# Experts of a mixture layer taken two at a time, each in one column half of the PE array

## The chip, the cores and the metric

The kernel runs on one core of one Trainium2 chip. The metric is the device time of one execution in microseconds; the median of three runs counts. All weights are read from HBM once, in fp32, 363.5 MB on the queue that carries them.

## What is computed

One layer: a token mixer (Fourier branch and a recurrent branch) and then an expert-choice feed-forward part, on 512 tokens of 1024 features. The change lies in the second part alone. Cut to that:

```python
def expert_choice_ffn(h, w_router, w_gate, w_up, w_down):
    cap = CAPACITY_FACTOR * T // N_EXPERTS                 # 2 * 512 / 16 = 64 tokens
    scores = softmax(einsum('btd,de->bte', h, w_router))
    g, idx = lax.top_k(swapaxes(scores, 1, 2), cap)        # each expert picks 64 tokens
    xg = h[idx]
    hid = silu(einsum('becd,edf->becf', xg, w_gate)) * einsum('becd,edf->becf', xg, w_up)
    out = einsum('becf,efd->becd', hid, w_down) * g[..., None]
    return zeros.at[idx].add(out)

x = x + g2 * expert_choice_ffn(modulate(rmsnorm(x, norm2_g), sh2, sc2), ...)
return rmsnorm(x, final_g)
```

There are 16 experts (NE). Each has w_gate and w_up of 1024 x 1536 and w_down of 1536 x 1024.

## The kernel before

The mixer and the router take the time up to some 468 us; the change leaves the order of their instructions as it is, but for one small copy on VectorE (csv) that is there so that the tile cs can live in a pool that closes early.

**Loads.** Each of the three matrices of an expert comes in eight units of 768 KB, 128 partitions x 1536 fp32 (6 KB a row). The list `units` (L827) gives their order: expert by expert, gate, up, down. `eload()` (L835) issues the next one on SP's queue; it goes into a ring of 22 buffers, 20 of three pools (NR = 14, 5, 1) and two lent from staging tiles (wd and we; `held`). A buffer is free when the matmuls that read its old contents are done, so each `eload()` stands right behind the products of a unit. SP's transfers take eight completion lanes in turn: a load is issued only when the one eight before it has landed, and copies that ACT issues take lanes of the same set. Expert 15's down matrix comes in nine smaller pieces (`LAST`, L829; L856): 512 columns in four pieces of three k blocks, then twice 256 columns in larger and smaller ones, which makes 2 KB and 1 KB a row.

**One expert** (loop at L1160). `up_gate` (L1108, products at L1116) multiplies the gathered tokens (xg, 64 columns as the stationary operand) by a unit, the two halves f of the 1536 columns in the two column halves of the PE array (tile_position (0, 64f)), each 384 columns at a time, into a two-bank PSUM tile, G or U. After each k a list of hooks runs other work: the scatter of the expert before (L1122, 1132), and the ranking of the expert after next (rank_a L1042, rank_d on VectorE, rank_p L1059 to 1069, rank_c L1071 to 1080). Silu (L1172, ScalarE) and the product with U (L1185, VectorE) follow; six transposes T (L1198), two copies to hT (L1199), and the down products Y (L1210), 512 columns in either half. After an odd expert the gather of the next two (`gather`, L1088, 64 matmuls of 128 columns) stands ahead of the transposes. For expert 0 the gather is spread: two pieces (`one_k`) ahead of the loop, the others and those of expert 1 in hooks. The gate row g2 is brought to the partitions it is needed on by two copies at expert 2 (L1190) and one at expert 14 (L1215), both on ACT's queue.

**PSUM.** G and U have two banks each, and four one-bank buffers ("a") serve everything else.

Of the kernel before, what the change touches and what calls it, by code (L numbers as in the profile page):

```python
# [76 lines left out]
def layer(ctx: ExitStack, tc: tile.TileContext, I, out):  # L77
# [54 lines left out]
    cs = keep.tile([P, KD, 32], F32, name="cs")  # L132
# [131 lines left out]
    def ada_acc(i):  # L264
        for j in ada_at.get(i, ()):
            raw = take("a", j)
            r = [stage.tile([P, 256], F32, tag="acc", bufs=2, name=f"acc{j}_{a}") for a in range(2)]
            m = len(r)
            for k in range(KD):
                if k < m:  # L270
                    dve.tensor_scalar(r[k], raw[:, k, :], cs[:, k, 0:1], None, op0=OP.mult)
                else:
                    dve.scalar_tensor_tensor(r[k % m], raw[:, k, :], cs[:, k, 0:1], r[k % m], op0=OP.mult, op1=OP.add)
# [36 lines left out]
    zs = st_p.tile([P, NT, 1028], F32, name="zs")  # L310
    rs, ce = zs[:, 0, 0:1024], zs[:, 1, 0:512]
# [523 lines left out]
    def eload():  # L835
# [5 lines left out]
        m, i = n % (sum(NR) + 2), 0  # L841
# [9 lines left out]
        if wn == "w_down_e":  # L851
            if e == NE - 1:
# [152 lines left out]
    for _ in range(NR[1]):  # L1005
# [8 lines left out]
    jk = wa[:, 2, P:P + 256].bitcast(BF16)  # L1014
    wb = stage.tile([P, 4, 512], F32R, tag="wH", bufs=2, name="wb")
    wc = stage.tile([P, 2048], F32, tag="wL", bufs=2, name="wc")
    wd = stage.tile([P, 2048], F32, tag="wH", bufs=2, name="wd")
    we = stage.tile([P, 2048], F32, tag="wL", bufs=2, name="we")
    held += [wd[:, 0:DE], we[:, 0:DE]]
    eload()  # L1020
    eload()
    g20 = we[:, DE:2048]
    sl = wc[:, 1280:2048]
    y = sl[:, 0:512]
    half = lambda t: t.bitcast(BF16)
    eq = lambda t: half(t).rearrange("p (n t) -> p n t", n=NT)
    RK = [(sB, [half(wc[:, 256 * c:256 * c + 256]) for c in range(NT)], eq(wc[:, 1024:1280])),
          (wa[:, 3, :], [half(sl[:, 256 * c:256 * c + 256]) for c in range(3)] + [half(wd[:, DE:DE + 256])],
           eq(wd[:, DE + 256:2048]))]
    oht = [wb[:, i, :] for i in range(3)]  # L1030
    yH = wb[:, 3, :]
    yL = [stage.tile([P, 256], F32R, tag="acc", bufs=2, name=f"yL{a}") for a in range(2)]
    hT = [t.rearrange("p (a b) -> p a b", a=3) for t in (wa[:, 3, 0:384], wd[:, DE:DE + 384])]
    xg = g1.rearrange("p (k c) -> p k c", k=KD)

    def at(name, shape=(P, 512)):
        return mps.tile(list(shape), F32, tag="a", bufs=4, name=name)

    def bcast(col4):
        a = at("bc")  # L1040
        for n in range(NT):
            pe.transpose(a[:, P * n:P * n + P], col4(n).to_broadcast([P, P]), ident)  # L1042
        return a

    def rank_a(e):
# [13 lines left out]
    def rank_p(e):  # L1059
        sB, GT, EQ = RK[e == 1]  # L1060
# [7 lines left out]
        h = CAP * (e % 2)  # L1068
        dve.tensor_tensor(oh[:, :, h:h + CAP], r.unsqueeze(2).to_broadcast([P, NT, CAP]),
                          iota0[:, None, :].to_broadcast([P, NT, CAP]), op=OP.is_equal)  # L1070

    def rank_c(e):
        sB, GT, EQ = RK[e == 1]
        a = at("rb")
        for c in range(NT - 1):
            pe.matmul(a, onesb, GT[c], start=c == 0, stop=False)
        for c in range(NT):
            pe.matmul(a[:, P * c:P * c + P], onesb, EQ[:, c, :], start=False, stop=False)
        pe.matmul(a, onesb, GT[NT - 1], start=False, stop=True)
        dve.tensor_scalar(oht[e % 3], a, pmod, None, op0=OP.is_equal)  # L1080
        dve.scalar_tensor_tensor(jk, oht[e % 3].bitcast(F32), 1.0, sB, op0=OP.mult, op1=OP.mult,
                                 accum_out=gc[:, e % 3:e % 3 + 1])

    h0, h1, hh = slice(0, CAP), slice(CAP, P), slice(0, P)

    def gather_k(a, k, q):
        for n in range(NT):
            pe.matmul(a[k // 4][:, P * (k % 4) + q.start:P * (k % 4) + q.stop], XN[n // 2][:, n % 2, P * k:P * k + P],  # L1088
                      oh[:, n, q], start=n == 0, stop=n == NT - 1)

    def gather_out_k(a, k, q):
        src = a[k // 4][:, P * (k % 4) + q.start:P * (k % 4) + q.stop]
        if k % 2 or k < 3 and q == h0:
            act.activation(xg[:, k, q], src, AF.Identity, bias=modc[:, 24 + k, 0:1], scale=s2[:, k:k + 1])
        else:
            dve.tensor_scalar(xg[:, k, q], src, s2[:, k:k + 1], modc[:, 24 + k, 0:1], op0=OP.mult, op1=OP.add)

    def gather():
        a = [at("xg0"), at("xg1")]
        for k in range(KD):  # L1100
            gather_k(a, k, slice(0, P))
        return a

    def gather_out(a, q):
        for k in range(KD):
            gather_out_k(a, k, q)

    def up_gate(e, wn, name, hooks):  # L1108
# [230 lines left out]
```

## Time and profile before

| | |
|---|---|
| runs | 1208.59, 1205.56, 1209.94 us, median 1208.59 |
| profiled execution | 1205.73 us, span 1203.9 us, mean granted clock 0.984 |
| busy, share of the span | PE 95%, VectorE 47%, ScalarE 24%, GpSimd 9% |
| transfers | 368 MB, mean 306 GB/s over the span |
| the experts | from the first product at 482.3 us to the last output |

In the page's forty slices (30 us each) the bandwidth is 356 GB/s in the slice from 570 us, then 418 to 422 in each up to 1140, 400 in the next and 211 in the last. TensorE is at 90% and more in nearly all slices, so the page's first line alone does not tell what the time hangs on. Rows are read as: line of the program, engine, operation, output <- inputs, shape, count, busy time. A matmul in fp32 leaves two records, so a product that the program writes once is counted twice.

### The profile page before, as it was taken

The page shows a single profiled execution, that of the slowest core. Times are in us where ns is not written, and L with a number is a line of the kernel's source. Part 1 is how long each engine was busy: PE and PEld are TensorE (multiplying, and loading weights), DVE is VectorE, ACT ScalarE, POOL GpSimd, SP SyncE. Part 2 cuts the span into 40 slices and gives each one's busy share as a digit, 9 for nine tenths or more (in the row PEclk, how much of TensorE's full clock was granted, in tenths as well). Part 3 has the DMA queues.
Part 4 walks back from the last instruction along what each step waited for, and adds up shares of the span by engine and source line. Part 5 has one row for each costly group of instructions (what it writes and reads, how often), then busy time and mean ns, then how long its engine had stood idle before and what let it go on. Part 6 is the DMA issues. An engine that isn't in the chain of part 4 may idle for free. (4 is left out here: it accounts for less than half of the span.)

```text
span 1203.9 us, 16716 instructions
## 1 busy us (share of the span) xinstructions
PE 1148.4 (95%) x6891; PEld 684.3 (57%) x6891; DVE 564.3 (47%) x1053; ACT 286.4 (24%) x448; POOL 112.9 (9%) x118
## 2 busy tenths in 40 slices
PE   8979988899999999999999999999999999999986
PEld 5768766588888897545445445445345345345333
DVE  5566899996776675233332332332232232232024
ACT  5443766644322223101001001001001001001004
POOL 5164443310000000000000000000000000000002
PEclk9989988999999999999999999999999999999998
DMA  8922011155555495899899999999999999999995
GB/s 308 300 89 88 18 53 53 35 173 177 188 180 191 149 390 206 313 379 418 356 422 419 418 420 421 418 419 421 420 417 421 421 418 418 422 421 418 419 400 211
DMA packets 115435, 368.01 MB, mean 306 GB/s; under 512 B 8912, under 2 KB 61656, under 8 KB 115232
## 3 DMA queue, kind: packets, MB, share of 16 engines
q1 hardware_dynamic: 112688, 363.52, 76.9%
q0 software_dynamic: 1088, 2.18, 0.6%
q10 hardware_dynamic: 1584, 1.25, 0.4%
q8 instruction: 54, 0.88, 0.3%
q14 instruction: 21, 0.17, 0.0%
HBM read 364.43 MB, written 2.10 MB: 304 GB/s over the span
## 5 line engine op out<-in xcount | busy, mean ns | idle before, releaser
L1116 PE MATMUL U<-ew,g 128*64 128x384 f32 x928 | 167.5, 494 | 8.7 <-DMA ew<-in_w_up_e 8.6
L1116 PE MATMUL G<-ew,g 128*64 128x384 f32 x960 | 171.7, 493 | 3.8 <-DMA ew<-in_w_gate_e 3.5
L1135 DVE TENSOR_TENSOR x<-x,sc 128x512 f32<-128x512 f32 x120 | 77.1, 684 | 104.2 <-PE sc L1132 104.2
L1116 PEld LDWEIGHTS G<-ew,g 128*64 128x64 f32 x960 | 62.8, 136 | 87.0 <-issue 62.6
L1116 PEld LDWEIGHTS U<-ew,g 128*64 128x64 f32 x928 | 60.0, 136 | 90.6 <-issue 56.9
L1247 POOL TENSOR_TENSOR o<-x,ew 128x512 f32<-128x512 f32 (+1 forms) x8 | 7.8, 1003 | 926.7 <-ACT o L1243 926.7
L1213 DVE SCALAR_TENSOR_TENSOR wc<-Y,gc,g 128x512 f32<-128x512 f32 x15 | 11.3, 751 | 148.6 <-PE Y L1210 148.6
L1210 PE MATMUL Y<-ew,wa 128*64 128x512 f32 x312 | 75.7, 598 | 2.2 <-ACT wa L1199 2.2
L1210 PE MATMUL Y<-ew,wd 128*64 128x512 f32 x324 | 77.5, 594 | 0.0
L1199 ACT COPY wa<-T 128x384 f32<-128x384 f32 x16 | 7.7, 479 | 254.2 <-PE T L1198 254.2
L230 DVE TENSOR_TENSOR wL<-raw,wH 128x1024 fp32r<-128x1024 f32 x48 | 62.9, 1341 | 2.0 <-ACT wH L229 1.6
L1172 ACT ACTIVATE wc<-G 128x768 f32<-128x768 f32 x16 | 13.0, 811 | 181.7 <-PE G L1116 181.7
L1210 PEld LDWEIGHTS Y<-ew,wd 128*64 128x64 f32 x324 | 24.2, 137 | 49.1 <-issue 41.7
L1088 PEld LDWEIGHTS xg<-wa,xn 128*128 128x128 f32 x448 | 51.1, 192 | 0.2
L1088 PE MATMUL xg<-wa,xn 128*128 128x128 f32 x448 | 51.2, 275 | 0.0
L1054 DVE TENSOR_SCALAR wc<-wa,score 128x128 bf16<-128x128 f32 (+3 forms) x63 | 24.0, 381 | 56.7 <-ACT wa L1047 56.7
L1210 PEld LDWEIGHTS Y<-ew,wa 128*64 128x64 f32 x312 | 21.8, 136 | 45.0 <-issue 34.6
L1216 ACT CAST wb<-wc 128x512 fp32r<-128x512 f32 x15 | 9.3, 619 | 156.1 <-DVE wc L1213 156.1
L674 PE MATMUL ga<-u,gw 128*128 128x512 f32 x64 | 36.0, 645 | 10.0 <-issue 9.9
L1132 PEld LDWEIGHTS sc<-wb 64*128 64x128 f32 x240 | 23.6, 184 | 35.9 <-issue 35.9
L229 ACT CAST wH<-raw 128x1024 fp32r<-128x1024 f32 x38 | 37.9, 1045 | 17.8 <-PE zO L426 9.9
L699 POOL TENSOR_TENSOR th<-tp,th 128x768 f32<-128x768 f32 x16 | 35.0, 2206 | 49.2 <-DVE tp L698 49.2
(360 smaller groups left out, 2183.9 us busy)
## 6 DMA issues: line engine op xcount, KB each, us to landing
ew<-in_w_gate_e SPq DMA_DIRECT2D x120, 768.0 KB, 14.9
ew<-in_w_up_e SPq DMA_DIRECT2D x116, 768.0 KB, 14.9
ew<-in_w_down_e SPq DMA_DIRECT2D x113, 768.0 KB, 14.9
raw<-in_w_ada SPq DMA_DIRECT2D x24, 1024.0 KB, 5.4
raw<-in_w_in SPq DMA_DIRECT2D x16, 1024.0 KB, 4.9
wd<-in_w_down_e SPq DMA_DIRECT2D x7, 768.0 KB, 12.3
we<-in_w_down_e SPq DMA_DIRECT2D x7, 768.0 KB, 12.9
wd<-in_w_up_e SPq DMA_DIRECT2D x6, 768.0 KB, 14.6
```

Of the source, the lines that this page charges most:

```text
L229: (copy or act.copy)(wH[:, a], raw[:, a])
L230: dve.tensor_sub(wL[:, a], raw[:, a], wH[:, a].bitcast(F32))
L674: pe.matmul(gf[:, 512:1024], gw[:, d, i, :], u[:, TC:TA], start=True, stop=True)
L699: pool.tensor_tensor(b, s, b, op=OP.mult)
L1054: dve.tensor_scalar(GT[c][:, 0:m], sB[:, 0:m], s, None, op0=OP.is_lt)
L1088: pe.matmul(a[k // 4][:, P * (k % 4) + q.start:P * (k % 4) + q.stop], XN[n // 2][:, n % 2, P * k:P * k + P], oh[:, n, q], start=n == 0, st ...
L1116: pe.matmul(t[64 * f:64 * f + 64, n, 0:384], xg[:, k, c:c + CAP], w[:, o:o + 384], start=k == 0, stop=k == KD - 1, tile_position=(0, 64 * f))
L1132: pe.matmul(a[dh][:, c], w, v, start=j == 0, stop=j == 1, tile_position=(64 * dh, 0))
L1135: dve.tensor_add(xs, xs, a[dh])
L1172: act.activation(v3(sl), G[:, :, 0:384], AF.Silu)
L1210: pe.matmul(yp[64 * dh:64 * dh + 64, :], hT[j // 3][:, j % 3, 64 * f:64 * f + 64], w[:, 512 * i:512 * i + 512], start=f == 0 and j == 0, s ...
L1213: dve.scalar_tensor_tensor(y, yp, gc[:, e % 3:e % 3 + 1], g2, op0=OP.mult, op1=OP.mult)
```

## The change

It takes the experts in pairs, p = 0 to 7, expert 2p in the lower and 2p + 1 in the upper column half.

- `units` alternates between the two experts of a pair, so a step of `up_gate` takes two units: three blocks of 512 columns for each expert. Each step issues two loads behind it. The ring has 21 buffers (we alone is lent).
- PSUM: six one-bank tiles (`mt`: three for G, three for U, then the two gather pieces, three for T, two for Y), two small ones (`at`).
- `rank_c` writes both experts of a pair into the two halves of one tile. The scatter sums both experts in one product over 128 partitions, 16 matmuls a pair of 512 columns.
- The gather of expert 0 stands as a whole ahead of the loop, and then rank_p(1) and two pieces for expert 1 (`gather_1`); the other six pieces are in the hooks of pair 0.
- The gate row copies: three on ACT's queue (`expand`) behind the gate products of pair 0; the late one is gone. The second column half of the gate row has a place of its own (g2b).
- `LAST` now holds for both experts of the last pair, 18 pieces instead of nine; the output part is adapted to it.

```diff
-    for e in range(NE):
-        units += [(e, wn, q) for wn in ("w_gate_e", "w_up_e", "w_down_e") for q in range(KD)]
+    for p in range(NE // 2):
+        units += [(2 * p + i, wn, q) for wn in ("w_gate_e", "w_up_e", "w_down_e") for q in range(KD) for i in range(2)]
...
-    units[-KD:] = [(NE, "final_g", 0)] + [(NE - 1, "w_down_e", (c0, cw, k0, nk)) for c0, cw, ks in LAST for k0, nk in ks]
+    units[-2 * KD:] = [(NE, "final_g", 0)] + [(NE - 2 + i, "w_down_e", (c0, cw, k0, nk))
+                                              for c0, cw, ks in LAST for k0, nk in ks for i in range(2)]
...
-        m, i = n % (sum(NR) + 2), 0
+        m, i = n % (sum(NR) + 1), 0
...
+    def mt(name):
+        return mps.tile([P, 512], F32, tag="m", bufs=6, name=name)
...
-    def up_gate(e, wn, name, hooks):
-        t = mps.tile([P, 2, 512], F32, tag=name, bufs=1, name=name)
-        c = CAP * (e % 2)
-        for k in range(KD):
-            w = EW.pop((e, wn, k))
-            for n in range(2):
-                for f in range(2):
-                    o = FH * f + 384 * n
-                    pe.matmul(t[64 * f:64 * f + 64, n, 0:384], xg[:, k, c:c + CAP], w[:, o:o + 384],
-                              start=k == 0, stop=k == KD - 1, tile_position=(0, 64 * f))
-            eload()
+    def up_gate(p, wn, name, hooks):
+        t = [mt(name) for _ in range(3)]
+        for k in range(KD):
+            w = [EW.pop((2 * p + i, wn, k)) for i in range(2)]
+            for b in range(3):
+                for i in range(2):
+                    pe.matmul(t[b][hf[i], :], xg[:, k, hf[i]], w[i][:, 512 * b:512 * b + 512],
+                              start=k == 0, stop=k == KD - 1, tile_position=(0, CAP * i))
+            eload()
+            eload()
...
+    def scatter(p, i):
+        n, dh = divmod(i, 2)
+        a = at("sc")
+        w = oht[p % 2][:, P * n:P * n + P]
+        for j, v in enumerate((yH[dh], yL[dh])):
+            pe.matmul(a, w, v, start=j == 0, stop=j == 1)
...
-    one_k(0, h0)
-    one_k(1, h0)
-    for e in range(NE):
+    g0 = mt("xg0")
+    for k in range(KD):
+        gather_k(g0[:, CAP * k:CAP * k + CAP], k, hf[0])
+    for k in range(KD):
+        xg_put(g0[:, CAP * k:CAP * k + CAP], k, hf[0], True)
+    rank_p(1)
+    gather_1(0)
+    gather_1(1)
+    for p in range(NP):
...
-            hooks[0] += [lambda: one_k(2, h0), lambda: rank_p(1)]
-            hooks[4].append(lambda: rank_c(0))
-            hooks[6].append(lambda: rank_c(1))
-            for k in range(3, KD):
-                hooks[k - 2].append(lambda k=k: one_k(k, hh))
+            for k in range(2, KD):
+                hooks[k - 2].append(lambda k=k: gather_1(k))
+            hooks[6].append(lambda: rank_c(0))
...
-        if e == 2:
-            for q in range(2):
-                nc.scalar.dma_start(g20[64 * q:64 * q + 64, :], g2[0:64, :])
+        if p == 0:
+            def expand():
+                for i in range(2):
+                    nc.scalar.dma_start(g2b[hf[i], :], g2[hf[1], :])
+                nc.scalar.dma_start(g2[hf[1], :], g2[hf[0], :])
+            hooks[0].append(expand)
+        Uu = up_gate(p, "w_up_e", "U", hooks)
...
-        if e == NE - 2:
-            nc.scalar.dma_start(g2[0:64, :], g2[64:128, :])
```

Three places in the order of instructions. The first is TensorE where the loop begins. Before (L1088 is the gather, xa a piece's PSUM tile, G the gate product of unit ew0):

```order
2014 L1141 MATMUL warm_3823<-onesb_87 128x512
2015 L1141 LDWEIGHTS onesb_87
2016 L1141 MATMUL warm_3823<-onesb_87 128x512
2017 L1088 MATMUL xa_3838<-wa_3345,xn2_0_3419 128x64 x2
2018 L1088 MATMUL xa_3838<-wa_3345,xn2_2_3596 128x64 x2
2019 L1088 MATMUL xa_3844<-wa_3345,xn2_0_3419 128x64 x2
2020 L1088 MATMUL xa_3844<-wa_3345,xn2_2_3596 128x64 x2
2021 L1116 MATMUL G_3850<-ew0_3168,g1_94 64x384 x4
```

Two pieces of the gather stand here between the warming matmuls and the first unit. Now, at the same place on TensorE, the end of what stands ahead of the first unit (L1068 is rank_p(1), L1094 the gather, and eight pieces of expert 0 stand ahead of that):

```order
2072 L1068 MATMUL rk_3884<-onesb_87,wb_3759 128x1
2073 L1094 MATMUL xa_3907<-wa_3347,xn2_0_3421 128x64 x2
2074 L1094 MATMUL xa_3907<-wa_3347,xn2_2_3598 128x64 x2
2075 L1094 MATMUL xa_3913<-wa_3347,xn2_0_3421 128x64 x2
2076 L1094 MATMUL xa_3913<-wa_3347,xn2_2_3598 128x64 x2
2077 L1113 MATMUL G_3919<-ew0_3170,g1_94 64x512
2078 L1113 MATMUL G_3919<-ew1_3172,g1_94 64x512
2079 L1113 MATMUL G_3920<-ew0_3170,g1_94 64x512
2080 L1113 MATMUL G_3920<-ew1_3172,g1_94 64x512
2081 L1113 MATMUL G_3921<-ew0_3170,g1_94 64x512
2082 L1113 MATMUL G_3921<-ew1_3172,g1_94 64x512
```

The first unit has moved from row 2021 to row 2077, and units ew0 and ew1, of the two experts, alternate in three blocks.

The second place is ACT's queue around the gate row copies, after the change (L1050 the copy of a rank's scores, L1171 Silu, g_95 the gate row g2, wc the tile that holds g2b):

```order
L1050 COPY wa<-bc 128x512
L1171 ACT_TABLE_LOAD
L1171 ACTIVATE wc<-G 128x512 x3
L1188 DMA wc<-g_95 64x512 x2
L1189 DMA g_95<-g_95 64x512
L1050 COPY wa<-bc 128x512
```

Before, two copies (L1190) stood behind the third expert's Silu and score copy, and one (L1215) behind the fifteenth's down product.

The third place is SP's queue at the end of the weights. Before:

```order
L847 DMA ew_7893<-in_final_g 128x1024
L856 DMA ew_7898<-in_w_down_e 128x3x512
L856 DMA ew_7903<-in_w_down_e 128x3x512
L856 DMA ew_7908<-in_w_down_e 128x3x512
L856 DMA ew_7913<-in_w_down_e 128x3x512
L856 DMA ew_7918<-in_w_down_e 128x6x256
L856 DMA ew_7930<-in_w_down_e 128x6x256
L856 DMA ew_7936<-in_w_down_e 128x6x256
L856 DMA ew_7954<-in_w_down_e 128x4x256
L856 DMA ew_7960<-in_w_down_e 128x2x256
```

Now the pieces of 512 columns are eight, and behind them stand these, two of each for the two experts:

```order
L859 DMA we<-in_w_down_e 128x6x256
L859 DMA ew_7242<-in_w_down_e 128x6x256
L859 DMA ew_7250<-in_w_down_e 128x6x256
L859 DMA ew_7252<-in_w_down_e 128x6x256
L859 DMA ew_7260<-in_w_down_e 128x6x256
L859 DMA ew_7262<-in_w_down_e 128x6x256
L859 DMA ew_7270<-in_w_down_e 128x4x256
L859 DMA ew_7272<-in_w_down_e 128x4x256
L859 DMA ew_7280<-in_w_down_e 128x2x256
L859 DMA ew_7282<-in_w_down_e 128x2x256
```

So the down matrix of expert 14, eight units of 1536 columns a row before, has moved into the list of small pieces.

## Rows read from the trace of the kernel before

**Rows 1.** Windows: stretch, us; busy PE, PEld, DVE, ACT, POOL; PEclk; DMA; GB/s

```profile
480.00:600.00 120.00, 119.49 (x822) 61.07 (x821) 38.37 (x95) 13.07 (x24) 0.00 (x0) 1.00 0.94 367
620.00:1140.00 520.00, 506.54 (x3262) 235.50 (x3258) 154.40 (x339) 43.33 (x82) 0.00 (x0) 1.00 1.02 420
1140.00:1160.00 20.00, 17.79 (x105) 6.67 (x106) 5.37 (x9) 1.43 (x2) 0.00 (x0) 1.00 1.01 403
1170.00:1175.00 5.00, 3.33 (x20) 1.57 (x18) 0.95 (x1) 0.81 (x2) 0.00 (x0) 1.00 1.02 383
1180.00:1185.00 5.00, 4.55 (x25) 2.26 (x25) 1.52 (x4) 0.62 (x1) 0.00 (x0) 1.00 0.96 311
```

**Rows 2.** The page's DMA issues: count, size, us from issue to landing

```profile
ew<-in_w_gate_e SPq DMA_DIRECT2D x120, 768.0 KB, 14.9
```

**Rows 3.** Timeline of PE at the loop's start: start us, us, instruction

```profile
479.38 0.24 PE L1065 MATMUL rk<-onesb,wc 128*128 128x1 bf16 x4
...
480.42 1.97 PE L1088 MATMUL xa<-wa,xn 128*128 128x64 f32 x16
482.32 1.51 PE L1116 MATMUL G<-ew,g 128*64 128x384 f32 x8
...
484.70 0.17 PE L1063 MATMUL rk<-onesb,wd 128*128 128x1 bf16 x1
...
485.28 1.51 PE L1116 MATMUL G<-ew,g 128*64 128x384 f32 x8
...
494.31 0.82 PE L1076 MATMUL rb<-wc,onesb 128*128 128x512 bf16 x3
...
495.40 1.05 PE L1088 MATMUL xa<-wa,xn 128*128 128x128 f32 x8
```

**Rows 4.** Timeline of PE, experts 2 to 4, last field in brackets: idle before

```profile
576.11 2.75 PE L1116 MATMUL G<-ew,g 128*64 128x384 f32 x16
...
649.23 2.79 PE L1210 MATMUL Y<-ew,wa 128*64 128x512 f32 x12 [0.17 <-ACT wa L1199]
...
659.59 2.75 PE L1116 MATMUL G<-ew,g 128*64 128x384 f32 x16
662.26 0.40 PE L1132 MATMUL sc<-wb 64*128 64x256 f32 x2
...
662.94 2.80 PE L1116 MATMUL G<-ew,g 128*64 128x384 f32 x16
```

**Rows 5.** Groups of PE instructions by line: busy us, mean ns | idle before

```profile
L1088 PE MATMUL xg<-wa,xn 128*128 128x128 f32 x448 | 51.2, 275 | 0.0
...
L1198 PE MATMUL T<-cst,wc 128*128 128x128 f32 x96 | 16.4, 307 | 2.3 <-DVE wc L1185 2.3
...
L1042 PE MATMUL bc<-cst,score 128*128 128x128 f32 x64 | 10.1, 284 | 0.1
```

**Rows 6.** SP's waits (us in total, times, longest), and SP's timeline from 580 us

```profile
SPq L861 <- DMA we<-g: 13.4, 1, 13.4
...
593.33 3.97 SPq L861 DMA_DIRECT2D ew<-in_w_gate_e  x8
```

**Rows 7.** Loads that SP issued from 496 to 504 us, line L861

```profile
DMA to landing us min/median/max: 4.1/4.1/4.3
```

**Rows 8.** The copies of L1190, that of L1215, and the page's Silu group

```profile
DMA to landing us min/median/max: 2.3/2.3/2.3
...
DMA to landing us min/median/max: 6.5/6.5/6.5
...
L1172 ACT ACTIVATE wc<-G 128x768 f32<-128x768 f32 x16 | 13.0, 811 | 181.7 <-PE G L1116 181.7
```

**Rows 9.** The last weight loads (L856), and DVE behind the last product

```profile
L856 SPq DMA_DIRECT2D ew<-in_w_down_e x9: 378/2518/3777, 1159.7 to 1181.4; - x9
...
DMA to landing us min/median/max: 7.8/12.5/14.7
...
1191.67 0.48 DVE L1274 SCALAR_TENSOR_TENSOR wc<-Y,gc,g 128x256 f32<-128x256 f32 x1 [1.04 <-PE Y L1267]
```

More of the change, by code (lines that the diff above doesn't have):

```diff
@@ L1030, in layer @@
[L1030 to L1033, printed above, removed]
+    RK = [(b, [half(wb[:, 1024 * i + 256 * c:1024 * i + 256 * c + 256]) for c in range(NT)], q)
+          for i, (b, q) in enumerate(((sB, eq(wa[:, 2, P:P + 256])), (wa[:, 3, :], eq(e1))))]
+    hT = wb[:, 0:DE].rearrange("p (a b) -> p a b", a=12)
@@ L1075, in rank_c @@
         for c in range(NT - 1):
-            pe.matmul(a, onesb, GT[c], start=c == 0, stop=False)
+            both(slice(0, T), lambda r: r[1][c], start=c == 0, stop=False)
         for c in range(NT):
[L1078 to L1082, printed above, removed]
@@ L1098, in gather @@
[L1098 to L1117 removed]
+            both(slice(P * c, P * c + P), lambda r: r[2][:, c, :], start=False, stop=False)
@@ new lines, in layer @@
+        if p:
+            for i in range(6):
+                hooks[2 + i].append(lambda i=i: scatter(p - 1, i))
+        else:
+            for k in range(2, KD):
+                hooks[k - 2].append(lambda k=k: gather_1(k))
+            hooks[6].append(lambda: rank_c(0))
+        nx = 2 * p + 2
+        if p + 1 < NP:
+            hooks[1 if p else 7].append(lambda: rank_a(nx))
+            for c in range(NT if p else 0):
+                hooks[2 + c].append(lambda c=c: rank_d(nx, c))
+            if p:
+                hooks[7].append(lambda: rank_p(nx))
@@ new lines, in layer @@
+        G = up_gate(p, "w_gate_e", "G", hooks)
+        for b in range(3):
+            act.activation(sl[:, 512 * b:512 * b + 512], G[b], AF.Silu)
+        hooks = {k: [] for k in range(KD)}
+        if p:
+            for i in range(2):
+                hooks[i].append(lambda i=i: scatter(p - 1, 6 + i))
+        elif p + 1 < NP:
+            for c in range(NT):
+                hooks[0].append(lambda c=c: rank_d(nx, c))
+            hooks[1].append(lambda: rank_p(nx))
+        if p + 1 < NP:
+            hooks[2].append(lambda: rank_a(nx + 1))
+            for c in range(NT):
+                hooks[3 + c].append(lambda c=c: rank_d(nx + 1, c))
+            hooks[7].append(lambda: rank_p(nx + 1))
@@ new lines, in layer @@
+        for a in range(3):
+            t = mt("T").rearrange("p (a b) -> p a b", a=4)
+            for b in range(4):
+                f, j = divmod(4 * a + b, 6)
+                pe.transpose(t[:, b, :], sl[:, FH * f + j:FH * f + FH:6], ident)
+            act.copy(hT[:, 4 * a:4 * a + 4, :], t)
+        if p == NP - 1:
+            break
+        Y = [mt("Y") for _ in range(2)]
+        for q in range(KD):
+            w = [EW.pop((2 * p + i, "w_down_e", q)) for i in range(2)]
+            f = q // 4
+            for b in range(3):
+                j, dh = divmod(3 * (q % 4) + b, 2)
+                for i in range(2):
+                    pe.matmul(Y[dh][hf[i], :], hT[:, 6 * f + j, hf[i]], w[i][:, 512 * b:512 * b + 512],
+                              start=f == 0 and j == 0, stop=f == 1 and j == 5, tile_position=(0, CAP * i))
+            eload()
+            eload()
@@ L1235, in out_a @@
         else:
-            for i in range(2):
-                c = slice(256 * i, 256 * i + 256)
-                pe.matmul(a[:, c], w, yH[:, c], start=True, stop=False)
-                pe.matmul(a[:, c], w, yL[i], start=False, stop=True)
+            pe.matmul(a, w, yH[0], start=True, stop=False)
+            pe.matmul(a, w, yL[0], start=False, stop=True)
         dve.tensor_add(x[:, n, cc], x[:, n, cc], a[:, 0:cw])
@@ L1302, in layer @@
     close_mps()
+    close_gx()
     close_rc()
```

200 lines of the change are left out of this document (82 added, 118 removed).

## The prediction

> **What bounds the kernel now.** The change touches only what follows 478 us: the sixteen experts. I read four things there, in this order. First the stretches of that part, with each engine's busy time and what the DMA moved. From 620 to 1140 us TensorE is busy 506.5 of 520 us and the DMA share is 1.02 at 420 GB/s [rows 1], so both look full, and the reader has to decide which one is. The second reading decides it: a weight load of 768 KB takes 14.9 us from issue to landing [rows 2], and at 420 GB/s one such load is 786,432 / 420,000 = 1.87 us of transfer; 14.9 is 8 × 1.87. Eight loads are in flight all the time, so nothing TensorE does makes them land sooner. Third, TensorE's own rate where it waits for nothing: the first product of expert 2 starts at 576.11 and that of expert 4 at 659.59 [rows 4], so a pair of experts is 83.5 us of TensorE, while its 48 loads are 48 × 1.87 = 89.8 us. TensorE is the faster of the two by 6 us a pair; it can only use up its lead and then wait. So the time of this part is: the moment from which the loads come without a gap, plus the bytes left divided by 420 GB/s, plus the tail behind the last landing. Fourth, where the loads do have gaps: 480 to 600 us moves 367 GB/s [rows 1]. The largest gap is a wait of 13.4 us on SP's queue for the gate row copies that ACT issues for expert 2 at 591 us, behind its own work, and SP goes on at 593.33 [rows 6, 8]. The load that then goes out is the 73rd (number 72, counted from 0), and lands about 4.1 us later [rows 7], at 597.4. Everything behind it follows at 1.87 us.
>
> **The change part by part.** I follow the loads through the new order.
>
> *Start.* The gather of expert 0 now stands whole ahead of the first product, and rank_p(1) and two pieces for expert 1 with it. One piece (eight matmul records of 64 columns) is 0.95 us: two took 480.42 to 482.32 [rows 3]. Eight are 7.6, so 480.42 becomes 488.0; rank_p 0.58 (484.70 to 485.28), 488.6; the hand-over from rank_p through DVE back to TensorE 0.80 (479.62, the end of the row of 479.38, to 480.42), 489.4; two more pieces 1.9: the first product starts at 491.3 instead of 482.32, 9 us later. Nothing hides this from TensorE; the loads feel it because all buffers are full and wait for the first to be freed.
>
> *First pair.* A step (two units, 12 records of 512 columns in two column halves) has its shape already in the down products: four of them took 649.23 to 659.59, 2.59 each [rows 4]. Gate products: 8 × 2.59 = 20.7, six gather pieces 5.7, one rank_c 1.09 (494.31 to 495.40) [rows 3], one rank_a 10.1 / 16 = 0.63 [rows 5]; they end at 519.4. The new rank_c sends its columns to two halves of the array; if these did not overlap it would be 2.2, and I take the overlap since the products' halves do. Up products: 20.7, rank_a 0.63 and two rank_p 1.16: 541.9. Then rank_c 1.09, the full gather 51.2 / 7 = 7.31, twelve transposes 2 × 16.4 / 16 = 2.05 [rows 5], a copy's 0.17 [rows 4]: 552.5. The first down step ends at 555.1 and frees buffers for loads 53 and 54 (units 32 and 33, 21 buffers on; one buffer fewer than before, since only one of the two staging tiles is still lent to the ring). Load 53 so lands at 555.1 + 4.1 = 559.2 at the earliest. By transfer alone: load 21 is issued when the first step ends, 493.9, lands at 498.0, and 32 more are 59.8: 557.8. The two nearly agree, so up to here the ring and the DMA are about even, and a gap in the loads is paid in full.
>
> *The copies on ACT's queue.* The new gate copies stand in pair 0 behind a table load and three Silus (0.81 us for 768 columns [rows 8], so about 0.54 each), and I put their issue at 522 to 524. Their completions lie in the same eight lanes as SP's loads: loads 38 and 39 wait for the first two and load 41 for the third, which itself waits for both. Behind these waits on SP stand all later loads; behind the third copy on ACT stands only the next rank's copy, which nobody needs before the end of the up products. A copy lands 2.3 to 6.5 us after issue [rows 8], so the first two at 525 to 530 and the third at 528 to 537. Load 38 has to leave by 525.7 not to be late (its landing by transfer alone is 498.0 + 17 × 1.87 = 529.8, less 4.1), load 41 by 531.3. Loss 0 to 6 us; I take 2.5, nearer to the 2.3 of the two copies of the same kind. Load 53 is then at 560.3 (559.2 to 563.8), load 72 at + 19 × 1.87 = 35.5, 595.8 (594.7 to 599.3), against 597.4 before. The old hold at 593 is gone, and **what is gained there the later start takes back**: −1.6 us (−2.7 to +1.9).
>
> *Last loads.* The down weights of expert 14 now come in small pieces as well, so 2 KB and 1 KB per partition and row instead of 6 KB. Half an expert's down matrix is 3.146 MB. In the trace the 2 KB pieces move at 383 GB/s (1170 to 1175) and the 1 KB pieces at 311 (1180 to 1185) [rows 1]: 8.2 + 10.1 = 18.3 us against 6.29 / 0.42 = 15.0: **+3.3 us**. If the 311 only shows fewer loads in flight at the end, the 2 KB half alone costs 0.7. I take 3.3, the rows as they are (0.7 to 3.3).
>
> [...]
>
> *The late gate copy* (issued at 1142.9, a row copied within g2) goes: 1140 to 1160 moved 403 GB/s instead of 420 [rows 1], 20 × 17 / 420 = −0.8 (−0.8 to 0).
>
> *Tail.* The last load was issued at 1181.4 and took 7.8: 1189.2; DVE reads the product at 1191.67 [rows 9], 2.5 us later. Afterwards the last two loads hold two k blocks of each expert, eight records of 256 columns: 2.59 × 256 / 512 × 8 / 12 = 0.9, with a hand-over 1.1. −1.3 (−1.4 to 0). The output behind it is the same work: nothing.
>
> *TensorE's saving.* Per pair: 24 steps 62.2, gather 7.31, transposes 2.2, ranks 3.5, scatters at most 8 × 0.68 = 5.4 (662.26 to 662.94 [rows 4]) and at least half: 78 to 81 instead of 83.5. It is worth nothing while loads set the pace: it becomes waiting for DMA.
>
> Sum: −1.6 + 3.3 − 0.8 − 1.3 = −0.4 us (−4.2 to +5.2). The profiled execution took 1205.73 (span 1203.9), so 1205.3 there; the median of the runs is 2.9 above it, hence **1208.2**.
>
> **The rivals.**
> A, the forecast: 1208.2, own range 1204.4 to 1213.8.
> B, TensorE is the bound. For it: 506.5 busy of 520 [rows 1]. Then 4.5 us × 8 pairs = 36 less, about 1172. Against it: the full queue of [rows 2] and a DMA share over 1 in the same row.
> C, slower: the ACT copies hold SP as long as before, 13.4 us [rows 6], now at a place where the ring has no backlog. Load 38 would leave at 521.9 + 13.4 = 535.3 and land at 539.4 instead of 529.8: 9.6 lost, load 53 at 567.4 and load 72 at 602.9, +5.5 in place of −1.6; the sum is +6.7, about 1215.3. It decides from a hold of some 12 us. For it: the same queues and lanes, and the third copy waits for two others. Against it: before, the copies stood far back on ACT when SP already waited; now ACT reaches them within 5 us of the end of the gate products.
> [...]
>
> **How the numbers follow.** A 0.76, B 0.06, C 0.12, D 0.06. A measurement of this kernel tells about 0.5%, 6 us, from no change. Faster by more than that (under 1202.5): B and a lower edge of A, 0.10. Slower (over 1214.6): most of C and an upper edge of A, 0.16. The rest, 0.74, is within. The range takes A's own and C: 1203 to 1216, leaving out B and the far ends of C.
>
> **What would show it.** Right: first product near 491, first down product near 553, loads 53 and 54 issued near 555; the 580 to 600 stretch at 420 GB/s and no wait of SP for a gate copy there, but a short one in 522 to 537; from 620 on 420 GB/s as before, with TensorE's idle time there grown from 13.5 us to some 35; under 400 GB/s for the last 34 us; the last landing near 1189 and an unchanged output behind it. Wrong: a pace of loads other than 1.87 us, TensorE without waits for DMA (B), a hold of over 12 us on SP in pair 0 (C), a granted clock under 1.00 between 700 and 1180 (D), or the small pieces at 420 GB/s.

## The result: 1.0% slower, and the loads run at another pace

| | before | after |
|---|---|---|
| median | 1207.49 us (4 runs) | 1219.09 us (1218.96 to 1221.66, 4 runs) |
| ratio | | 1.0102, 95% interval 1.0081 to 1.0123 |
| profiled execution | 1205.73, span 1203.9 | 1219.05, span 1217.3 |

The time is 3.1 us above the upper end of the range (1216.0), on the side to which the forecast gave 0.16. Of the runs below, one execution of a_early took 1849.83 us at a granted clock of 0.555, and its row leaves it out. The windows of the changed kernel, with the columns of [rows 1], and its DMA issues, as [rows 2]:

```profile
480.00:600.00 120.00, 118.29 (x700) 55.87 (x698) 29.15 (x81) 13.22 (x28) 0.00 (x0) 0.97 0.88 348
485.00:490.00 5.00, 4.20 (x54) 4.13 (x54) 0.58 (x2) 1.58 (x6) 0.00 (x0) 1.00 0.02 5
490.00:495.00 5.00, 5.00 (x23) 3.04 (x24) 0.34 (x1) 1.29 (x5) 0.00 (x0) 0.56 0.00 0
495.00:500.00 5.00, 5.00 (x24) 1.95 (x22) 0.34 (x1) 0.00 (x0) 0.00 (x0) 0.76 0.27 60
620.00:1140.00 520.00, 500.47 (x2577) 211.70 (x2574) 117.23 (x273) 43.11 (x82) 0.00 (x0) 1.00 1.02 415
...
1180.00:1185.00 5.00, 3.14 (x14) 1.02 (x16) 0.00 (x0) 0.00 (x0) 0.00 (x0) 1.00 1.00 330
...
ew<-in_w_gate_e SPq DMA_DIRECT2D x123, 768.0 KB, 15.1
```

Three things are to be seen. **The long stretch** from 620 to 1140 us moves 415 GB/s, where [rows 1] has 420, with the same DMA share of 1.02; a load takes 15.1 us instead of 14.9 [rows 2]. The forecast had 1.87 us a load on both sides of the change. The share cannot tell the two apart: the engines are as busy, only slower. **The start** moves 348 GB/s instead of 367: from 485 to 497 us nothing is in flight, and the granted clock is 0.56 from 490 to 495. **The end** is as slow as [rows 1] has it, for longer.

Followed by the loads (issue and landing of each are in the trace), the 13.3 us between the two spans lie so:

| stretch | before | after | difference | forecast |
|---|---|---|---|---|
| to the issue of load 18 (last but two of the first filling) | 470.28 | 471.22 | +0.9 | 0 |
| from there to the landing of load 90 | 162.06 | 168.32 | +6.3 | −1.6 |
| to the issue of load 360 | 494.61 | 499.53 | +4.9 | 0 |
| to the last landing | 62.25 | 63.55 | +1.3 | +2.5 |
| to the end of the span | 14.72 | 14.65 | −0.1 | −1.3 |

The first row is not the change's: over the runs below it lies between 469.4 and 472.9 without order. The other rows are counted from load 18 for that reason.

The start in the changed kernel, TensorE's timeline (to be read against [rows 3]):

```profile
481.02 7.36 PE L1094 MATMUL xg<-wa,xn 128*128 128x64 f32 x64
...
489.66 2.78 PE L1094 MATMUL xa<-wa,xn 128*128 128x64 f32 x16 [0.81 <-DVE wa L1071]
492.38 5.29 PE L1113 MATMUL G<-ew,g 128*64 128x512 f32 x12
497.60 1.10 PE L1094 MATMUL xa<-wa,xn 128*128 128x64 f32 x8
498.63 2.79 PE L1113 MATMUL G<-ew,g 128*64 128x512 f32 x12
```

The first product comes at 492.38 (forecast 491.3), but its step takes 5.29 us and the next one 2.79, and the two pieces of the gather ahead of it 2.78 instead of the 1.97 of [rows 3]: the granted clock is 0.50 from 490.6 to 497.4 us. Then the waits on SP's queue and the timelines of ACT and SP in pair 0, as [rows 6]:

```profile
SPq L862 <- DMA g<-g: 5.9, 1, 5.9
SPq L862 <- DMA wc<-g: 5.2, 2, 3.9
...
524.69 0.52 ACTq L1188 DMA_DIRECT2D wc<-g  x1
...
525.25 0.61 ACTq L1188 DMA_DIRECT2D wc<-g  x1
...
533.24 0.47 ACTq L1189 DMA_DIRECT2D g<-g  x1
...
540.02 0.33 SPq L862 DMA_DIRECT2D we<-in_w_down_e  x1
```

The copies go out at 524.7 and 525.2, the third when both have landed, at 533.2, and SP issues load 41 at 540.0. The old wait of 13.4 us is gone, as forecast; three shorter ones stand in its place.

### The profile page after: what moved, and what is told of

Read it like the earlier page. It is cut to its first block, busy times and chain, and to the rows that moved or that the text cites. A ratio compares the mean times of both kernels' runs of the same rounds, so it can differ in the third digit from the quotient of the medians.

```text
span 1217.3 us, 14957 instructions
## 1 busy us (share of the span) xinstructions
PE 1151.3 (95%) x6064; PEld 658.7 (54%) x6067; DVE 515.1 (42%) x972; ACT 287.3 (24%) x452; POOL 112.8 (9%) x118
## 5 line engine op out<-in xcount | busy, mean ns | idle before, releaser
L1113 PE MATMUL U<-ew,g 128*64 128x512 f32 x732 | 187.6, 600 | 16.8 <-DMA ew<-in_w_up_e 16.8
L1113 PE MATMUL G<-ew,g 128*64 128x512 f32 x738 | 194.0, 607 | 1.7 <-DMA ew<-in_w_gate_e 1.7
L1218 PE MATMUL Y<-ew,wb 128*64 128x512 f32 x636 | 145.7, 593 | 4.9 <-ACT wb L1208 4.9
L1128 DVE TENSOR_TENSOR x<-x,sc 128x512 f32<-128x512 f32 x56 | 38.5, 687 | 182.1 <-PE sc L1126 182.1
L1218 PEld LDWEIGHTS Y<-ew,wb 128*64 128x64 f32 x636 | 47.3, 137 | 93.4 <-issue 86.0
L1094 PE MATMUL xg<-wa,xn 128*128 128x128 f32 (+1 forms) x512 | 59.2, 276 | 0.0
L1094 PEld LDWEIGHTS xg<-wa,xn 128*128 128x128 f32 x512 | 57.8, 192 | 2.3 <-issue 1.8
L1098 ACT ACTIVATE g<-xg,modc,s 128x128 f32<-128x128 f32 (+1 forms) x36 | 15.3, 448 | 185.3 <-DVE g L1100 174.1
L1171 ACT ACTIVATE wc<-G 128x512 f32<-128x512 f32 x24 | 14.1, 597 | 142.3 <-PE G L1113 142.3
L1126 PEld LDWEIGHTS sc<-wd,oht 128*128 128x128 f32 x112 | 16.6, 188 | 45.4 <-issue 45.4
L1126 PE MATMUL sc<-wd,oht 128*128 128x512 f32 x112 | 41.0, 447 | 0.0
L273 DVE SCALAR_TENSOR_TENSOR acc<-raw,csv,acc 128x256 f32<-128x256 f32 x96 | 39.3, 475 | 0.0
## 6 DMA issues: line engine op xcount, KB each, us to landing
ew<-in_w_gate_e SPq DMA_DIRECT2D x123, 768.0 KB, 15.1
ew<-in_w_up_e SPq DMA_DIRECT2D x122, 768.0 KB, 15.1
ew<-in_w_down_e SPq DMA_DIRECT2D x119, 768.0 KB, 15.1
we<-in_w_up_e SPq DMA_DIRECT2D x6, 768.0 KB, 15.1
```

The source lines that it names most:

```text
L273: dve.scalar_tensor_tensor(r[k % m], raw[:, k, :], csv[:, k:k + 1], r[k % m], op0=OP.mult, op1=OP.add)
L1094: pe.matmul(o, XN[n // 2][:, n % 2, P * k:P * k + P], oh[:, n, q], start=n == 0, stop=n == NT - 1)
L1098: act.activation(xg[:, k, q], o, AF.Identity, bias=modc[:, 24 + k, 0:1], scale=s2[:, k:k + 1])
L1113: pe.matmul(t[b][hf[i], :], xg[:, k, hf[i]], w[i][:, 512 * b:512 * b + 512], start=k == 0, stop=k == KD - 1, tile_position=(0, CAP * i))
L1126: pe.matmul(a, w, v, start=j == 0, stop=j == 1)
L1128: dve.tensor_add(xs, xs, a)
```

## Experiments

The names: those that begin with a_ are the changed kernel with an edit, those with b_ the kernel before with an edit. "Start" is from the issue of load 18 to the landing of load 90, in the one traced execution. The medians are of different sessions, and each ratio is to the kernel before in the same session, so two runs compare best by their ratios.

| run | median us | ratio to before (95%) | GB/s 620 to 1140 | start us |
|---|---|---|---|---|
| before | 1205.98 to 1207.49 | 1 | 420 | 162.1 |
| after | 1219.09 | 1.0081 to 1.0123 | 415 | 168.3 |
| a_seq | 1221.04 | 1.0093 to 1.0128 | 415 | 168.1 |
| a_early | 1216.35 | 1.0053 to 1.0091 | 415 | 164.7 |
| a_copy | 1218.42 | 1.0066 to 1.0102 | 415 | 165.4 |
| a_warm | 1216.38 | 1.0073 to 1.0111 | 415 | 166.7 |
| a_big14 | 1218.48 | 1.0064 to 1.0106 | 415 | 168.4 |
| b_mis | 1214.38 | 1.0032 to 1.0073 | 415 | 162.4 |
| a_align | 1202.68 | 0.9954 to 0.9989 | 424 | 164.6 |
| b_align | 1199.90 | 0.9914 to 0.9958 | 424 | 161.6 |
| b_align64 | 1205.29 | 0.9980 to 1.0001 | 420 | 161.8 |
| a_best | 1193.15 | 0.9849 to 0.9920 | 424 | 157.8 |
| b_best | 1194.31 | 0.9883 to 0.9925 | 423 | 155.9 |

### Is the slower pace the two address streams? (a_seq)

The change lets loads alternate between two experts' matrices, which lie 6 MiB apart. The edit keeps every buffer and every place in the program and gives load n the source that load n of the kernel before has:

```diff
+    nfull = 368
+    srcq = [(e, wn, q) for e in range(NE) for wn in ("w_gate_e", "w_up_e", "w_down_e") for q in range(KD)]
...
+        EW[e, wn, q] = t
+        if n < nfull:
+            e, wn, q = srcq[n]
         src = I[wn][0, e]
```

> The changed kernel; each of its 368 full weight loads goes to the same buffer at the same place of the program, but reads the 768 KB that the kernel before reads in that place: expert by expert, eight units of a matrix in a row. The computation is changed by it: units are multiplied with the wrong expert's weights. It asks where the pace of 415 GB/s (before: 420) from 620 to 1140 us comes from. Theory (two address streams, 6 MiB apart, cost bandwidth): that stretch is back at 420 to 421 GB/s and the time falls by about 6 us, 520 x 5 / 415. Rival (it comes from the core: 21 buffers, two loads issued at a time, 512-column products that read the buffers): 415 as in the changed kernel, the same time.

Measured: 415 GB/s, 1221.04 us. The theory falls; the order of the sources costs nothing that shows. That leaves the core's side of the loads.

### Is it the place of the buffers in SBUF? (a_align, b_mis)

One line of the diff had been read as free: the tile cs, 1024 bytes a partition, leaves the long-lived pool, and csv with 32 bytes takes its place. Every tile allocated behind it on that side moves down by 992 bytes, which is four times 256 less 32. In the built program the ring buffers of the kernel before begin, counted past a multiple of 256 bytes, at 0 (six of the ring and the two lent ones) and at 224 (the 14 of the other side); in the changed kernel at 32 (seven) and at 224 (14). None is on the grid of 256 any more. That 256 bytes is the grid that counts was an assumption of mine, which the runs here and in the next part test. Two edits, in opposite directions, neither of which touches an instruction's work:

```diff
 a_align
-    csv = keep.tile([P, KD], F32, name="csv")
+    csv = keep.tile([P, 64], F32, name="csv")[:, 0:KD]
...
+    pad, close_pad = sb("pad", "right")
+    pad.tile([P, 56], F32, name="padr")
     rings[0], close_ra = sb("ra", "right")
```

```diff
 b_mis
     cs = keep.tile([P, KD, 32], F32, name="cs")
+    keep.tile([P, 8], F32, name="padl")
```

> The changed kernel, with nothing but its tiles' places in SBUF moved: 224 bytes of padding left of the ring buffers and 224 right of them, so that all 21 buffers begin at a multiple of 256 bytes in their partitions (before this run: none of them, 7 lie at 32 and 14 at 224 past one; in the kernel before the change 8 of 22 lay at 0 and 14 at 224). Theory (a load into a buffer off that grid is slower; the change moved the last aligned ones off it by making one small tile 992 bytes shorter): from 1.870 us a load with 8 of 22 aligned and 1.895 with none, an aligned one takes 1.826, so 620 to 1140 us moves about 430 GB/s and the time falls by some 20 us, below the kernel before. Rival (21 buffers, loads issued in twos, or TensorE's wider products set the pace): 415 GB/s and the same time.

> The kernel before the change with 32 bytes of padding behind one small tile: its 8 aligned ring buffers move to 32 past a multiple of 256 bytes, and nothing else of the program is changed. Theory (place of the buffers): 415 GB/s instead of 420 in 620 to 1140 us, time up by 6 to 9 us. Rival: 420 and no change.

The windows of 620 to 1140 us, first of b_mis and then of a_align:

```profile
620.00:1140.00 520.00, 503.44 (x3231) 234.12 (x3240) 155.56 (x341) 43.28 (x82) 0.00 (x0) 1.00 1.02 415
```

```profile
620.00:1140.00 520.00, 502.58 (x2624) 222.26 (x2622) 119.33 (x276) 43.69 (x82) 0.00 (x0) 1.00 1.02 424
```

Both came on the theory's side: 32 bytes of padding make the kernel before slower by 8.4 us between the medians (1214.38 against 1205.98; by the ratio, 1.0053, 6.4 us, and 3.9 to 8.8 by its interval), with the changed kernel's 415 GB/s and nothing of its change; 448 bytes make the changed kernel 16.4 us faster than it was (15.8 by the ratios), and faster than the kernel before. The rate with all buffers on the grid is 424, not the 430 that I had worked out: the 8 buffers moved from 0 to 32 cost more than their share, and the 14 moved from 224 to 0 brought less. The rival, that the number of buffers, the issue in twos or TensorE's wider products set the pace, is out: each of the two kernels has both paces.

### The same in the kernel before, and how fine the grid is (b_align, b_align64)

The edit is the pad on the right side alone, 224 bytes in b_align and 32 bytes in b_align64.

> The kernel before the change with 224 bytes of padding ahead of its 14 ring buffers on the right side: all 22 buffers begin at a multiple of 256 bytes. Theory (place of the buffers): some 430 GB/s in 620 to 1140 us until TensorE, which needs 83.5 us a pair against 48 x 1.826 = 87.7, is nearly the bound as well; the time falls by 10 to 16 us. Rival: 420 and no change.

> The kernel before the change with 32 bytes of padding ahead of its 14 ring buffers on the right side: they begin at 192 past a multiple of 256 bytes, which is a multiple of 64, and the other 8 at 0 as before. Theory A (a grid of 64 bytes is enough): 424 GB/s from 620 to 1140 us and about 1200 us, as with all buffers on the grid of 256. Theory B (the grid is 256 or more): 420 GB/s or less, about 1206.

First b_align, then b_align64:

```profile
620.00:1140.00 520.00, 508.94 (x3283) 238.66 (x3292) 156.43 (x342) 43.41 (x83) 0.00 (x0) 1.00 1.02 424
```

```profile
620.00:1140.00 520.00, 506.54 (x3255) 236.24 (x3264) 154.41 (x339) 43.32 (x82) 0.00 (x0) 1.00 1.02 420
```

With the 14 buffers at 192 past a multiple of 256, which is on a grid of 64, the rate is that of the kernel before, and the time the same within the interval. So a grid of 64 bytes isn't enough here (420 GB/s), and one of 256 is (424). A grid of 128 was not tried.

### The start: clock, order, copies (a_warm, a_early, a_copy)

a_warm asks whether the clock of the first step, 0.50 from 490.6 to 497.4 us, hangs on the small products ahead of it. It puts ten warming products among them, four behind rank_p(1):

```diff
         gather_k(g0[:, CAP * k:CAP * k + CAP], k, hf[0])
+        if k == 4:
+            warm2(4)
...
     rank_p(1)
+    warm2(4)
     gather_1(0)
+    warm2(2)
     gather_1(1)
```

> The changed kernel with ten warming products of 512 columns (bf16) put among the gather of expert 0, behind rank_p(1) and between the two pieces of expert 1; nothing else is moved. [...]

```profile
485.00:490.00 5.00, 4.87 (x55) 4.05 (x55) 0.81 (x3) 2.48 (x8) 0.00 (x0) 1.00 0.01 3
490.00:495.00 5.00, 4.99 (x31) 2.74 (x30) 0.12 (x1) 0.41 (x1) 0.00 (x0) 1.00 0.01 1
...
490.18 1.10 PE L1094 MATMUL xa<-wa,xn 128*128 128x64 f32 x8
491.21 2.80 PE L1113 MATMUL G<-ew,g 128*64 128x512 f32 x12
493.94 1.10 PE L1094 MATMUL xa<-wa,xn 128*128 128x64 f32 x8
```

The granted clock stays at 1.00 and TensorE's timeline shows the first step at 2.80 us: with ten products more, the first load behind it goes out 1.8 us earlier and load 90 lands 1.6 us earlier (both counted from load 18). The median is 2.7 lower, but the intervals of the two ratios overlap. So the fall of the clock is real and cost some 1.6 us by the loads, and with ten wide products among the small ones it did not come. Whether the small products alone set it off is not shown: the warming products also fill the wait of 0.81 us for VectorE, which may as well be the cause. In a_early that wait is gone and the clock falls all the same (0.68 from 485 to 490 us, 0.63 from 490 to 495), but two waits of 0.5 us for ScalarE stand there instead.

a_early lets only four pieces of expert 0's gather and two of expert 1's stand ahead of the loop:

```diff
-    for k in range(KD):
+    for k in range(4):
+        if k == 3:
+            rank_p(1)
         gather_k(g0[:, CAP * k:CAP * k + CAP], k, hf[0])
-    for k in range(KD):
         xg_put(g0[:, CAP * k:CAP * k + CAP], k, hf[0], True)
-    rank_p(1)
...
-                hooks[k - 2].append(lambda k=k: gather_1(k))
+                hooks[k - 2].append(lambda k=k: (gather_1 if k < 4 else gather_2)(k))
```

> The changed kernel with a shorter way to the first product: only four pieces of expert 0's gather and two of expert 1's stand ahead of it, with rank_p(1) behind the third so that the fourth covers the hand-over to VectorE; the last four pieces of both experts are gathered together in the hooks. Theory (the late first unit, and with it an idle DMA, 5 GB/s or less from 485 to 495 us, is the main loss): the first product comes near 487.3 instead of 492.4, its step lasts 2.7 instead of 5.3 because the clock holds at 1.00, the first load behind it goes out near 490 instead of 497.7, and the time falls by 6 to 8 us. Rival (the copies or TensorE's pace in pair 0 hold the loads later anyway): the first loads come earlier, but load 80, issued at 604.5 in the changed kernel, moves by less than 2 us.

```profile
484.87 0.17 PE L1066 MATMUL rk<-onesb,we 128*128 128x1 bf16 x1
...
486.46 3.27 PE L1094 MATMUL xa<-wa,xn 128*128 128x64 f32 x16
489.67 4.76 PE L1118 MATMUL G<-ew,g 128*64 128x512 f32 x12
```

Only part of it came: the pieces share one PSUM tile, and two of them wait 0.5 us each for ScalarE; the clock falls all the same (4.76 us for the step), so the first product is at 489.67, not 487.3. Counted from load 18, load 80 goes out 2.6 us earlier and load 90 lands 3.6 us earlier. The median is 2.7 lower, where 6 to 8 were expected, and the intervals of the two ratios overlap. (gather_2 is gather_1 with the columns of both experts.) By the loads the theory is right in kind and too large in size, and the rival (load 80 moves by less than 2 us) is out.

a_copy puts the three gate copies on SP's queue behind the first filling of the ring:

```diff
     g2f = [g2, g2b]
+    g2h = [slice(CAP * i, CAP * i + CAP) for i in range(2)]
+    for i in range(2):
+        nc.sync.dma_start(g2b[g2h[i], :], g2[g2h[1], :])
+    nc.sync.dma_start(g2[g2h[1], :], g2[g2h[0], :])
...
-                    nc.scalar.dma_start(g2b[hf[i], :], g2[hf[1], :])
-                nc.scalar.dma_start(g2[hf[1], :], g2[hf[0], :])
```

> The changed kernel with its three gate row copies on SP's queue ahead of the first product, behind the last load of the first filling, instead of on ACT's queue in pair 0. Theory (the waits of SP for these copies cost 2 to 4 us): the waits for them at 531 to 540 us are gone, 525 to 545 us moves about 410 GB/s instead of 340 to 386, and the time falls by 2 to 4 us. Rival (other loads are in flight meanwhile, so the waits are hidden): load 80 and the time stay within 1 us.

The window of 520 to 545 us, first of the changed kernel, then of a_copy:

```profile
520.00:545.00 25.00, 25.00 (x148) 9.16 (x146) 8.95 (x29) 4.03 (x6) 0.00 (x0) 1.00 1.00 374
```

```profile
520.00:545.00 25.00, 25.00 (x148) 9.01 (x146) 8.95 (x29) 4.03 (x6) 0.00 (x0) 1.00 1.02 414
```

40 of 414 GB/s in 25 us are 2.4 us; load 90 lands 2.9 us earlier. The median is only 0.7 lower, with an interval of 0.2% either side that doesn't tell the two readings apart.

### The end: do expert 14's short rows cost it? (a_big14)

The pieces keep size and order; expert 14's are read as one run a partition:

```diff
+                off = {0: 0, 512: 6144, 768: 9216}[c0] + k0 * cw
+                f, j = divmod(off, 6144)
+                u = t[:, 0:cw * nk]
...
+                if e == NE - 2:
+                    nc.sync.dma_start(u, src[FH * f:FH * f + FH, :].rearrange("(p k) d -> p (k d)", k=6)[:, j:j + cw * nk])
```

> The changed kernel in which the small pieces of expert 14's down matrix keep their size and order but are read from HBM as one run of up to 6 KB a partition. The computation is changed by it: expert 14's down products get the wrong weights. Theory (short runs cost bandwidth): the stretch from the first small piece's issue (1155 us) to the last landing (1202.6) shortens by about 3.3 us, as in the forecast's term. Rival (the low rate there comes from fewer bytes in flight at the end): within 1 us of the changed kernel.

Landing times of the small pieces, those of the changed kernel, then expert 15's in a_big14:

```profile
DMA to landing us min/median/max: 7.0/12.9/14.8
```

```profile
DMA to landing us min/median/max: 8.5/14.6/16.1
```

From the first small piece's issue (1156.1 in both) to the last landing it takes 45.95 us instead of 46.51: 0.6, not 3.3; the rival's number. But its reason is not shown either. With expert 14's rows long, 1180 to 1195 us moves 378, 356 and 340 GB/s in steps of 5 us instead of 330, 303 and 335, so short rows do cost rate; the last piece, of expert 15, goes out 2.0 us earlier (1193.56 instead of 1195.60) and then takes 8.5 us instead of 7.0 to land. What is gained on the way is given back by the last pieces, which are short in both. The traced span is no shorter either (1217.8 against 1217.3): in a_big14 the granted clock is 0.66 from 1190 to 1195 us, where the changed kernel has 1.00, and the last products, which wait 0.90 us for a load in the changed kernel, wait for none there: TensorE is the later of the two. From load 360, behind which both kernels have the same bytes left, to the last landing the changed kernel takes 63.55 and b_mis, at the same pace, 62.52: the whole new end up to the last landing, the missing late copy included, costs 1.0 us.

### Both repaired (a_best, b_best)

a_best joins a_align, a_copy and a start with two pieces of either expert ahead of the first product and warming products between them. b_best joins b_align with its two gate copies (L1190) on SP's queue ahead of the first product:

```diff
 b_best
     g20 = we[:, DE:2048]
+    for q in range(2):
+        nc.sync.dma_start(g20[64 * q:64 * q + 64, :], g2[0:64, :])
...
-            for q in range(2):
-                nc.scalar.dma_start(g20[64 * q:64 * q + 64, :], g2[0:64, :])
```

> The changed kernel with all 21 buffers aligned, the three gate copies on SP's queue ahead of the first product, and a shorter start: two pieces of either expert's gather ahead of the first product, with warming products of 512 columns between them and behind rank_p(1), the other pieces for both experts together in the hooks. Theory (buffers' places, start and copies add up): 430 GB/s from 620 us on, clock 1.00 in the first step of the gate products, which begins near 488 and lasts 2.7 us, and some 1190 us in all, 16 below the kernel before. Rival (place of the buffers does nothing): 1212 to 1215.

> The kernel before the change, one expert at a time, with all 22 buffers at multiples of 256 bytes and its two gate row copies of expert 2 put on SP's queue ahead of the first product. It asks how much of a faster version needs the pairs. Theory (the pairs themselves bring nothing while loads set the pace): the wait of 13.8 us of SP is gone, the stretch from 590 to 595 us is back from 79 to 424 GB/s, and the time is 4 to 6 us under that with aligned buffers alone, 1194 to 1196, within 3 us of the pairs with the same repairs. Rival (TensorE, with 83.5 us a pair against 48 x 1.855 = 89.0, becomes the bound here, and the pairs with their 79 do not): over 1198.

The window of 590 to 595 us, where the old hold had left the DMA idle, and the long stretch, first of b_align, then of b_best:

```profile
590.00:595.00 5.00, 5.00 (x34) 2.03 (x30) 1.05 (x4) 1.40 (x2) 0.00 (x0) 1.00 0.35 136
```

```profile
590.00:595.00 5.00, 5.00 (x36) 2.28 (x34) 1.87 (x5) 1.40 (x2) 0.00 (x0) 1.00 1.01 423
620.00:1140.00 520.00, 510.00 (x3317) 241.34 (x3326) 158.10 (x346) 43.95 (x83) 0.00 (x0) 1.00 1.02 423
```

a_best is 3 us over what was expected and b_best inside it; they lie within 1.2 us of each other, which the intervals do not tell apart: 1193.15 (0.9849 to 0.9920 of the kernel before) in pairs, 1194.31 (0.9883 to 0.9925) one expert at a time. Either beats both kernels that were compared. The pairs save TensorE 1.5 us of work a pair (82.0 against 83.5, shown in the next section), and the loads don't ask for it.

## Why the prediction was wrong

The forecast for the traced execution was −0.4 us and the spans differ by +13.3. Of these 13.7 us, 7.9 lie in the start, 4.9 in the pace of the loads behind it, 1.2 in the tail and 0.9 ahead of load 18; the last loads came 1.2 better than forecast.

**The step that failed first** is "Everything behind it follows at 1.87 us", taken over to the changed kernel, and with it the edit that was costed at nothing, cs and csv. The prediction took a load's 1.87 us for a property of the transfer. It was a mean over buffers on the grid of 256 bytes and off it (1.864 and 1.867 us in the runs with all of them on it, 1.909 and 1.911 with none), and the change put them all off it. By the loads this is +4.9 us between loads 90 and 360; in b_mis, the same displacement without the rest, the same stretch is +6.5, and the median +8.4 where the whole change has 11.6. (Of the 1.6 us between the two stretches 1.3 are one gap in b_mis: loads 349 and 350 go out 3.2 us apart instead of 1.9. What made it is not shown.) The place of the buffers bears on the start too: with all of them on the grid (a_align) it is 164.6 us instead of 168.3; how much of that is the displacement by 32 bytes was not separated. The prediction did name "a pace of loads other than 1.87 us" as what would prove it wrong, and it is the first thing that the profile after shows.

**The start**, the larger miss, was forecast at −1.6 and is +6.3. The frame of it was right: the first product at 492.4 (491.3 expected), the old hold gone, the first loads and the copies' waits as the two bounds, and both were paid in full. Three terms were too small. The first step was costed at 2.59 and took 5.29, because the granted clock fell to 0.50 ahead of it (490.6 to 497.4 us), and a_warm, where it does not fall, has 2.80. D of the chances is a granted clock under 1.00 between 700 and 1180 us; there, in the starved steps, it stays at 1.00, and on until 1210.8; of the runs, only a_align (0.75 from 1170 to 1175 us, 0.91 from 1175 to 1180) and a_big14 (0.66 from 1190 to 1195) show it lower, for 3.4 us among the last small pieces. A copy was put at 2.3 to 6.5 us from issue to landing and the three took 6.7, 7.9 and 6.7, each above that: at 593 us, where [rows 8] has the 2.3, the queue stood empty because of the hold itself (101 GB/s from 591.0 to 593.3 us in the kernel before, with the two copies alone in flight), so that row was the wrong one of the two. The third landed at 540.0 (528 to 537 expected); the loss, forecast at 2.5, is 2.4 to 2.9 by a_copy. And a step of pair 0 with its piece is 3.76 us, not 3.54, so that the first down product came at 558.3 instead of 552.5 and loads 53 and 54 left at 561.1 instead of 555.1.

**The last loads** were forecast at +3.3 for rows of 2 KB and 1 KB, and a_big14 gives them 0.6. The rows at 383 and 311 GB/s [rows 1] were read rightly, short rows are slower (1180 to 1185 us moves 330 GB/s in the changed kernel and 378 in a_big14); but more bytes at that rate were added up as if the last landing moved by the sum, and in a_big14 it moved by 0.6, though half of the pieces came in long rows. The low end that the prediction kept, 0.7, was the better value.

**The late copy**, −0.8, lies in the same stretch and was not measured by itself; both together are +1.0 against b_mis, where +2.5 was forecast. **The tail**, −1.3, did not come: VectorE reads the last product 2.3 us after the last landing (1202.62 to 1204.93; [rows 9] have 2.5), and the rest to the end of the span is unchanged. The forecast let eight records follow the last landing; TensorE ran 24 in a row there, from 1202.07 on (2.8 us): the last pieces landed at 1201.2, 1201.9 and 1202.6, and a scatter (from 1201.01) stood ahead of their products.

**TensorE's saving** became waiting, as forecast. Of its waits from 620 to 1140 us in the changed kernel

```profile
PE U L1113 <- DMA ew<-in_w_up_e: 13.0, 17, 0.8
PE G L1113 <- DMA ew<-in_w_gate_e: 1.7, 3, 0.8
```

these 14.7 us are for loads; its idle time there is 19.5 us (520 less 500.47) instead of 13.5, less than the 35 that I had put. The saving itself was mis-sized. The gate products of the second and third pair begin here, with no wait for a load between them:

```profile
578.95 5.32 PE L1113 MATMUL G<-ew,g 128*64 128x512 f32 x24
...
660.98 5.32 PE L1113 MATMUL G<-ew,g 128*64 128x512 f32 x24
```

A pair takes TensorE 82.0 us, not 78 to 81, against 83.5 before. And the busy time holds some of the waiting: a gate step is 2.80 us at 588.16 and 3.19 at 847.26, where the loads set the pace. Rival B is out by a_align: TensorE's work is unchanged, and the time follows the loads. Rival C's mechanism was there at a smaller size, 5.2 and 5.9 us of waits against the 12 from which it would have decided.

## What to carry to other kernels

Where loads set the pace, look at where their buffers begin: two paddings of 224 bytes were worth 16 us here, while the rewritten expert loop brought nothing that shows, since its saving became waiting. A small tile that goes from an early pool shifts everything behind it (here by 992 bytes). A DMA share of 1.02 stood beside 415, 420 and 424 GB/s here, so it doesn't tell the pace; compare GB/s in the same stretch. A saving on an engine that waits was worth nothing here, and when such a change moves the time, look first at what it did to the transfers by accident.

## What the runs showed of the hardware

- A load of 768 KB in rows of 6 KB took 1.864 and 1.867 us with all buffers at multiples of 256 bytes (a_align and b_align, 424 GB/s), 1.888 with 8 of 22 there (before, 420) and 1.909 and 1.911 with none (after and b_mis, 415), by a straight line through the landings of loads 95 to 344, with an unchanged share of busy DMA time, 1.02. (The 1.87 of the prediction divides by a rate that holds other transfers too.) Starts at 192 past the grid are nearly as slow as starts at 224 (14 of 22 buffers in either case: b_align64 1.884, before 1.888). The runs agree with a grid of 256 bytes for the place written to; what makes it is not shown. By an estimate from these times the displacements cost unlike amounts: the 8 buffers at 32 0.023 × 22 / 8 = 0.063 us each, 3.4% (b_mis less before), and the 14 at 224 0.021 × 22 / 14 = 0.033, 1.8% (before less b_align).
- In the changed kernel TensorE's granted clock was 1.00 from 231.2 to 490.6 us, 0.50 from 490.6 to 497.4, and 1.00 again from there to 1210.8. Ahead of the fall stood only products of 64 columns and of one (481.0 to 490.6), with a wait of 0.81 us among them; the 0.50 lasted through the first wide step (5.29 us), and was gone in the second (2.79 us). With ten products of 512 columns among the small ones and in that wait it stayed at 1.00 (a_warm, 480 to 500 us; first step 2.80 us). In the starved steps from 620 to 1140 us, 0.96 of the time busy, with waits of up to 0.8 us, it stayed at 1.00. In a_big14 it fell at 1190.1 us for 3.4 us (0.66 from 1190 to 1195), among the last small pieces and behind waits of up to 1.5 us; the changed kernel has such a wait too, 1.52 us, and kept 1.00 there.
- A copy of 128 KB within SBUF took 2.3 us from issue to landing with nothing else in flight [rows 8]; among loads in flight the three of the changed kernel took 6.7, 7.9 and 6.7 us (landings at 531.4, 533.2 and 540.0).
